# Two chained matmuls with a GELU: the opening's loads as eight of 512 KB, with a cast and turned by pairs of contraction slices

## The chip, the cores and the metric

The kernel runs on one core of one Trainium2 chip. The metric is the device time of one execution in microseconds (us); the kernel before is given by the median of 11 runs, 123.88 us (lowest 123.28, highest 124.94).

## The reference

a is 1024 x 1024, b is 1024 x 2048, c is 2048 x 1024, all float32.

```python
h = np.matmul(a, b)
h = 0.5 * h * (1 + np.tanh(np.sqrt(2 / np.pi) * (h + 0.044715 * h ** 3)))
return np.matmul(h, c).astype(np.float32)
```

## The kernel before, in words

TensorE contracts over the 128 partitions, so both operands need the contraction index there. b has it so as it lies in memory. a has its rows there, and must be turned: 128 x 128 blocks go through TensorE against an identity matrix into a PSUM bank, and VectorE copies them out to aT. The product is kept transposed: `hT[h][:, t]` is the GELU of 128 columns of b (tile t of 16) against 512 rows of a (half h of 2). The contraction has eight slices of 128 (k = 0 to 7).

The first product is computed in two parts. Its tiles t = 0 to 7 are plain bf16 matmuls (`mm1`, L109 to L112; each has 128 x 128 weights from b and 512 columns of aT). Its tiles 8 to 15, and the whole second product with c, go through `seven`, a seven-product scheme of sums and differences in float32r. Nothing of `seven` is changed here; it follows the part that is.

**The opening** is everything before the sixteen plain tiles can run freely. Slices k = 0 to 3 of a and of b's first 1024 columns are fetched in float32 by SyncE's queue into the staging buffers sta and stb, and cast to bf16 on the chip. All the rest (a's slices 4 to 7, called a2; b's slices 4 to 7; the second half of b; c) is fetched by GpSimd's queue, which casts to bf16 on the way. GpSimd's queue is held back by the gate (L81): a copy of one element of stb, which can only run when the load that brings this element has landed, and GpSimd takes its work in order.

The parts that matter here, in the order in which each engine gets them (the schedule is written out by hand, and every engine runs its own list in order):

- SyncE: sixteen loads of 256 KB with rows of 2 KB. Four of a (half 0, one block of 128 rows each, 512 columns), b's slices 0 and 1 (columns 0 to 511, called c = 0), four of a (half 1), b's slices 2 and 3, and then b's slices 0 to 3 for columns 512 to 1023 (c = 1). The gate reads slice 3, c = 0: the twelfth load.
- `turn1(h, fill)` (L125 to L137): for each block m of 128 rows, cast (VectorE for even m, ScalarE for odd), four transposes into bank 4 + m, a few small matmuls on zeros (`stir`, L119 to L123), and copies of 128 x 512 to aT. Only after all four blocks is aT for that half complete, for all four slices at once.
- `cast_b(k, c)` (L139 to L142): ScalarE casts one slice of b to b1.
- The plain matmuls of tiles 0 to 3: half 0 with slices 0 and 1 (8), `turn1(1)`, half 1 with slices 0 and 1 (8), and then both halves with slices 2 and 3 (16): 32 in all, in banks 0 to 7. Then `half` (L162 to L167): ScalarE and VectorE copy the eight partial sums to SBUF, in turn.
- T2 (L238 to L251): tiles 4 to 7 of both halves, in banks 0 to 6, first with slices 0 to 3, then tile by tile with slices 4 to 7 and the GELU. Between the first ones, four `turn` calls transpose a2 into bank 7 (L173), and VectorE copies it out (L174). A T2 tile can start when its bank has been copied to `half`, and needs the c = 1 columns of b1.

Behind that stand the second halves of tiles 0 to 3 (L254 to L259), and `seven` twice.

Of the kernel before, what the change touches and what calls it, by code (L numbers as in the profile page):

```python
# [9 lines left out]
F32 = mybir.dt.float32  # L10
F32R = mybir.dt.float32r
BF16 = mybir.dt.bfloat16
AF = mybir.ActivationFunctionType
# [6 lines left out]
def kernel(ctx, tc, a, b, c, out):  # L20
    nc = tc.nc
# [3 lines left out]
    H = 512  # L25
    KT = K // 128
    NT = N // 128

    av = a.rearrange("(mt p) k -> p mt k", p=128)
    bv = b.rearrange("(kt p) n -> p kt n", p=128)  # L30
# [9 lines left out]
    def slot(tag, shape, dt, name):  # L40
        return big.tile(shape, dt, name=name, tag=tag)

    def bank(i, shape=(128, H), dt=F32, name="ps"):
        return pp.tile(list(shape), dt, name=name, tag=f"bank{i}", padded_shape=None)

    def pieces(tag, bufs, shape, dt, name):
        return small.tile(shape, dt, name=name, tag=tag, bufs=bufs)
# [3 lines left out]
    ident = consts.tile([128, 128], BF16, name="ident")  # L51
    make_identity(nc, ident)
    gate = consts.tile([128, 1], F32, name="gate")
# [4 lines left out]
    aT = slot("a", [128, 2, KT, H], BF16, "aT")  # L58
    b1 = slot("b1", [128, KT, 1024], BF16, "b1")
# [1 line left out]


    KH = KT // 2
    stb = slot("x0", [128, 4, 1024], F32, "stb")
    sta = slot("x1", [128, 2, 4, H], F32, "sta")

    def load_a(h, m):
        nc.sync.dma_start(out=sta[:, h, m], in_=av[:, 4 * h + m, 0:H])  # L68

    def load_b(k, c):  # L70
        nc.sync.dma_start(out=stb[:, k, ts(c, H)], in_=bv[:, k, ts(c, H)])

    for h in range(2):
        for m in range(4):
            load_a(h, m)
        load_b(2 * h, 0)
        load_b(2 * h + 1, 0)
    for k in range(KH):
        load_b(k, 1)

    nc.gpsimd.tensor_copy(gate, stb[:, 3, 0:1])  # L81
    nc.scalar.activation(g, warm[:, 0:1], AF.Gelu_apprx_tanh)
    wps = bank(7, name="warmps")
    for _ in range(7):
# [11 lines left out]
    for n in range(2):  # L96
        for k in range(0, KT, 4):
            nc.gpsimd.dma_start(out=b2[:, k:k + 4, ts(n, H)],
                                in_=bv[:, k:k + 4, ds(1024 + n * H, H)])
# [3 lines left out]
    def copy(eng, dst, src):  # L103
        if eng is nc.scalar:
            nc.scalar.activation(dst, src, AF.Copy)
        else:
            nc.vector.tensor_copy(dst, src)  # L107

    def mm1(p, t, h, ks, k0=0, k1=KT):  # L109
        for k in ks:  # L110
            nc.tensor.matmul(p, b1[:, k, ts(t, 128)], aT[:, h, k],  # L111
                             start=(k == k0), stop=(k == k1 - 1))  # L112

    def gelu(t, h, p):
        nc.scalar.activation(hT[h][:, t], p, AF.Gelu_apprx_tanh)  # L115

    ps = {(0, t): bank(t) for t in range(4)}

    def stir(n):  # L119

        for _ in range(n):
            nc.tensor.matmul(ps[0, 3][:, 0:128], warm[:, 0:128], warm[:, 0:128],
                             start=True, stop=True, skip_group_check=True)  # L123

    def turn1(h, fill):  # L125
        pts = []
        for m in range(4):
            ab = pieces("ab", 4, [128, H], BF16, "ab")
            copy(nc.scalar if m % 2 else nc.vector, ab, sta[:, h, m])
            pt = bank(4 + m, (128, KH, 128), BF16, "pt")  # L130
            for k in range(KH):
                nc.tensor.transpose(pt[:, k], ab[:, ts(k, 128)], ident)  # L132
            stir(fill[m])
            pts.append(pt)
            if m in (0, 2, 3):
                for q in ((0,), (), (1, 2), (3,))[m]:
                    nc.vector.tensor_copy(aT[:, h, 0:KH, ts(q, 128)], pts[q])  # L137

    def cast_b(k, c, n=1):  # L139
        for i in range(n):  # L140
            r = ds(c * H + i * (H // n), H // n)
            nc.scalar.activation(b1[:, k, r], stb[:, k, r], AF.Copy)  # L142

    turn1(0, (2, 0, 4, 5))
    for k in range(2):
        cast_b(k, 0, 2 - k)
        for t in range(4):
            mm1(ps[0, t], t, 0, (k,), 0, KH)
    turn1(1, (0, 0, 0, 0))
    for t in range(4):  # L150
        ps[1, t] = bank(4 + t)
    for k in range(2):
        for t in range(4):
            mm1(ps[1, t], t, 1, (k,), 0, KH)
    for k in range(2, KH):
        cast_b(k, 0)
        for h in range(2):
            for t in range(4):
                mm1(ps[h, t], t, h, (k,), 0, KH)


    half = slot("x3", [128, 2, 4, H], F32, "half")  # L162
    for k in range(KH):
        cast_b(k, 1)
    for h in range(2):
        for t in range(4):
            copy(nc.vector if t % 2 else nc.scalar, half[:, h, t], ps[h, t])  # L167

    def turn(h, m, i):
        pt = bank(i, (128, KH, 256), BF16, "pt")  # L170
# [67 lines left out]
    T2 = [(h, t) for h in range(2) for t in range(4, 8)]  # L238
# [4 lines left out]
            turn(n // 4, 2 * (n % 2), 7)  # L243
    one.t3()
    one.t2()
    for h, t in T2[:7]:
        mm1(ps[h, t], t, h, range(KH, KT))
        gelu(t, h, ps[h, t])
    p = bank(7)
    mm1(p, 7, 1, range(KT))  # L250
# [3 lines left out]
    for n in range(8):  # L254
        h, t = divmod(n, 4)
# [156 lines left out]
```

## Time and profile before

| | |
|---|---|
| median of 11 runs | 123.88 us |
| profiled execution, whole time | 124.3 us |
| its span (first to last instruction) | 122.5 us |
| TensorE busy | 113.3 us, 92% |
| VectorE / ScalarE / GpSimd busy | 87.9 / 55.1 / 14.8 us |
| mean granted TensorE clock | 0.984 |
| read from HBM / written | 20.97 MB / 4.19 MB |

The profile counts from the span's start. Groups of instructions are named by line, engine and operation, with output and input by the program's names. PE is TensorE's matmul side, PEld its weight load, DVE VectorE, ACT ScalarE, POOL GpSimd, SPq SyncE's DMA queue. In a timeline a row is a run of like instructions: start, length, what it is, and in brackets how long the engine had been idle and what ended that. In a table by stages each row is a stretch of time with each engine's busy time in it, the granted clock (PEclk, 1.00 is full speed), the mean share of the DMA engines' time and the bytes moved. TensorE's matmuls are pipelined: a 512-column matmul is listed with 379 ns or more, but follows the one before it after 216 ns at full clock, and after 427 ns at half clock; a transpose after 56 or 107 ns.

### The profile page before, as it was taken

To read this page: it belongs to the slowest core of one execution; us is meant where nothing else is said; L and a number is where in the kernel's file an instruction comes from. 1 tells how busy PE (TensorE), PEld (TensorE's weight loads), DVE (VectorE), ACT (ScalarE), POOL (GpSimd) and SP (SyncE) were. 2 spreads that over 40 slices of the span, in tenths; PEclk is the share of its full clock that TensorE was granted. 3 is DMA by queue.
4 is the path that set the end of the run, shared out by engine and by line. 5 is a ranking of instruction groups with operands and counts; after the bars stand their busy time and mean duration, and the time that the engine had idled before them with its cause. 6 is when DMAs were issued, how large, how long until landed. Compare 5 with 4: busy or idle time off the path is not lost.

```text
span 122.5 us, 1463 instructions
## 1 busy us (share of the span) xinstructions
PE 113.3 (92%) x540; PEld 72.8 (59%) x546; DVE 87.9 (72%) x97; ACT 55.1 (45%) x89; POOL 14.8 (12%) x27
## 2 busy tenths in 40 slices
PE   6849599999999999999999999999999999999970
PEld 2333344455444444688888544458888888888850
DVE  0251606948805799979669999969999997792490
ACT  4225956001745688956579634920003596100000
POOL 2000597444223100000000000000000000000000
PEclk9995999999999999999999999999999999999999
DMA  3799999999999999998000000044000001004595
GB/s 118 243 265 400 340 136 198 166 196 205 207 206 213 211 209 212 212 211 166 8 3 0 5 0 0 0 172 171 0 0 0 0 5 76 10 0 171 215 354 201
DMA packets 10566, 16.86 MB, mean 138 GB/s; under 512 B 832, under 2 KB 3904, under 8 KB 10560
## 3 DMA queue, kind: packets, MB, share of 16 engines
q0 software_dynamic: 5952, 8.39, 39.6%
q1 hardware_dynamic: 4608, 8.39, 19.3%
q8 instruction: 4, 0.07, 0.2%
q14 instruction: 2, 0.02, 0.0%
HBM read 20.97 MB, written 4.19 MB: 205 GB/s over the span
## 4 chain that ended last, share of the span: by engine, by line
PE 71%; DVE 11%; DMA 10%; issue 2%; SPq 1%; ACT 1%; DVEq 0%; ACTq 0%
PE ps L227 49%; PE ps L111 20%; DVE x L185 6%; DMA stb<-in_b_dram 5%; DMA out_dram<-ot 5%; DVE ot L273 2%; DVE half L107 2%; SPq L68 1%; PE pt L173 1%; DVE aT L137 1%; DVE ot L358 1%; PE pt L132 1%; DVE aT L174 0%; ACT u L268 0%; DVE ab L107 0%
## 5 line engine op out<-in xcount | busy, mean ns | idle before, releaser
L111 PE MATMUL ps<-aT,b 128*128 128x512 bf16 x125 | 30.1, 394 | 1.6 <-ACT b L142 0.9
L227 PE MATMUL ps<-x,s 128*128 128x512 f32 x128 | 29.6, 391 | 0.0
L227 PEld LDWEIGHTS ps<-x,s 128*128 128x128 f32 x128 | 24.0, 188 | 5.1
L111 PEld LDWEIGHTS <-b 128*128 128x128 bf16 x128 | 12.6, 101 | 16.4 <-issue 2.1
L227 PE MATMUL ps<-x,x 128*128 128x512 f32 x64 | 14.8, 389 | 0.0
L227 PE MATMUL ps<-c_sb,hT 128*128 128x512 bf16 x62 | 13.9, 379 | 0.1
L227 PEld LDWEIGHTS ps<-x,x 128*128 128x128 f32 x64 | 12.0, 188 | 2.5
L268 ACT ACTIVATE v<-ps 128x512 f32<-128x512 f32 x8 | 4.8, 599 | 17.1 <-PE ps L227 17.1
L115 ACT ACTIVATE hT<-ps 128x512 bf16<-128x512 f32 x12 | 6.8, 594 | 11.4 <-PE ps L111 11.4
L227 PE MATMUL ps<-x 128*128 128x512 f32 x48 | 11.3, 394 | 0.0
L227 PEld LDWEIGHTS <-hT 128*128 128x128 bf16 x64 | 6.2, 98 | 7.6 <-issue 0.3
L227 PEld LDWEIGHTS ps<-x 128*128 128x128 f32 x48 | 9.0, 188 | 2.0
L258 DVE TENSOR_TENSOR half<-ps,half 128x512 f32<-128x512 f32 x8 | 5.5, 692 | 5.5 <-PE ps L111 5.1
L185 DVE TENSOR_TENSOR x<-c_sb 128x1024 fp32r<-128x1024 bf16 x8 | 9.2, 1216 | 0.0
L273 DVE TENSOR_TENSOR ot<-ps,v 128x512 f32<-128x512 f32 x8 | 5.3, 686 | 4.6 <-DMA out_dram<-ot 3.8
L273 DVE TENSOR_TENSOR ot<-ps,u 128x512 f32<-128x512 f32 x8 | 5.3, 690 | 3.1 <-ACT u L268 3.1
L115 ACT ACTIVATE hT<-ot 128x512 bf16<-128x512 f32 x12 | 6.9, 624 | 1.1 <-DVE ot L273 1.1
L227 PE MATMUL ps<-aT,b 128*128 128x512 bf16 x31 | 7.0, 379 | 0.1
L101 POOL DMA_DIRECT2D c_sb<-in_c_dram x8 | 5.7, 713 | 11.0 <-DMA b<-in_b_dram 11.0
L268 ACT ACTIVATE p<-ps 128x512 f32<-128x512 f32 x8 | 4.7, 594 | 4.9 <-PE ps L227 4.9
L137 DVE COPY aT<-pt 128x512 bf16<-128x512 bf16 x8 | 3.3, 421 | 4.5 <-PE pt L132 4.5
L115 ACT ACTIVATE hT<-half 128x512 bf16<-128x512 f32 x8 | 5.0, 631 | 2.6 <-DVE half L258 2.6
(47 smaller groups left out, 117.5 us busy)
## 6 DMA issues: line engine op xcount, KB each, us to landing
c_sb<-in_c_dram POOLq DMA_DIRECT2D x8, 512.0 KB, 19.9
out_dram<-ot SPq DMA_DIRECT2D x16, 256.0 KB, 2.1
sta<-in_a_dram SPq DMA_DIRECT2D x8, 256.0 KB, 5.9
stb<-in_b_dram SPq DMA_DIRECT2D x8, 256.0 KB, 5.9
b<-in_b_dram POOLq DMA_DIRECT2D x4, 512.0 KB, 14.6
a<-in_a_dram POOLq DMA_DIRECT2D x4, 256.0 KB, 5.3
b<-in_b_dram POOLq DMA_DIRECT2D x4, 256.0 KB, 9.5
```

The costliest lines, as they stand in the source:

```text
L68: nc.sync.dma_start(out=sta[:, h, m], in_=av[:, 4 * h + m, 0:H])
L101: nc.gpsimd.dma_start(out=c_sb[:, t:t + 2], in_=cv[:, t:t + 2])
L107: nc.vector.tensor_copy(dst, src)
L111: nc.tensor.matmul(p, b1[:, k, ts(t, 128)], aT[:, h, k], start=(k == k0), stop=(k == k1 - 1))
L115: nc.scalar.activation(hT[h][:, t], p, AF.Gelu_apprx_tanh)
L132: nc.tensor.transpose(pt[:, k], ab[:, ts(k, 128)], ident)
L137: nc.vector.tensor_copy(aT[:, h, 0:KH, ts(q, 128)], pts[q])
L185: nc.vector.tensor_tensor(out=dst[:, r], in0=x[:, r], in1=y[:, r], op=op)
L227: nc.tensor.matmul(p[:, ds(c0, w)], l[:, k, ts(j, 128)], r[:, k, ds(c0, w)], start=(start and k == 0), stop=(k == self.kt - 1), skip_group ...
L258: nc.vector.tensor_tensor(out=half[:, h, t], in0=p, in1=half[:, h, t], op=ADD)
L268: nc.scalar.activation(st, p, AF.Copy)
L273: nc.vector.tensor_tensor(out=ot, in0=p, in1=st, op=ADD)
```

## The change

SyncE makes eight loads of 512 KB in place of sixteen of 256 KB. A load of a brings all four row blocks of a half for two contraction slices (256 columns: rows of 1 KB); a load of b brings two slices (rows of 2 KB). Their order: a half 0 slices 0 and 1; b slices 0 and 1; a half 1 slices 0 and 1; a half 0 slices 2 and 3; b slices 2 and 3; a half 1 slices 2 and 3; then the two loads of b's c = 1. I number them 1 to 8. The gate reads b's slice 3, c = 0, as before: now load 5.

a is cast in one instruction of 128 x 1024 per load (three on VectorE, one on ScalarE), turned by eight transposes into one bank, and copied out in one instruction of 128 x 1024. aT is so ready by pairs of slices. The matmuls of tiles 0 to 3 follow in that order: half 0 with slices 0 and 1 (8), half 1 tiles 0 to 2 with slice 0 (3) and 1 (3), half 0 with slices 2 (4) and 3 (4), half 1 tiles 0 to 2 with slices 2 and 3 (6), and half 1's tile 3 with all four (4), since bank 7 serves the turns until then. Half 0's sums leave for `half` before the last ten matmuls, on ScalarE behind all four casts of c = 1. In T2, the second parts of the first four tiles run slice by slice over the four tiles, not tile by tile.

The loads, the gate and the opening (the diff's core; the functions `load_a`, `load_b`, `cast_a`, `turn1`, `block` and `leave` are new or rewritten):

```diff
-    stb = slot("x0", [128, 4, 1024], F32, "stb")
-    sta = slot("x1", [128, 2, 4, H], F32, "sta")
-    def load_a(h, m):
-        nc.sync.dma_start(out=sta[:, h, m], in_=av[:, 4 * h + m, 0:H])
-    def load_b(k, c):
-        nc.sync.dma_start(out=stb[:, k, ts(c, H)], in_=bv[:, k, ts(c, H)])
-    for h in range(2):
-        for m in range(4):
-            load_a(h, m)
-        load_b(2 * h, 0)
-        load_b(2 * h + 1, 0)
-    for k in range(KH):
-        load_b(k, 1)
-    nc.gpsimd.tensor_copy(gate, stb[:, 3, 0:1])
+    stb = slot("x0", [128, 2, KH, H], F32, "stb")
+    sta = slot("x1", [128, 2, 2, 4, 256], F32, "sta")
+    def load_a(h, q):
+        nc.sync.dma_start(out=sta[:, h, q], in_=av[:, 4 * h:4 * h + 4, ds(q * 256, 256)])
+    def load_b(q, c):
+        nc.sync.dma_start(out=stb[:, c, 2 * q:2 * q + 2], in_=bv[:, 2 * q:2 * q + 2, ts(c, H)])
+    load_a(0, 0)
+    load_b(0, 0)
+    load_a(1, 0)
+    load_a(0, 1)
+    load_b(1, 0)
+    load_a(1, 1)
+    load_b(0, 1)
+    load_b(1, 1)
+    nc.gpsimd.tensor_copy(gate, stb[:, 0, 3, 0:1])
...
-    def turn1(h, fill):
-        pts = []
-        for m in range(4):
-            ab = pieces("ab", 4, [128, H], BF16, "ab")
-            copy(nc.scalar if m % 2 else nc.vector, ab, sta[:, h, m])
-            pt = bank(4 + m, (128, KH, 128), BF16, "pt")
-            for k in range(KH):
-                nc.tensor.transpose(pt[:, k], ab[:, ts(k, 128)], ident)
-            stir(fill[m])
...
+    def cast_a(h, q, eng):
+        ab = pieces("ab", 2, [128, 4, 256], BF16, "ab")
+        copy(eng, ab, sta[:, h, q])
+        return ab
+    def turn1(h, q, i, ab):
+        pt = bank(i, (128, 2, H), BF16, "pt")
+        for n in range(2):
+            for m in range(4):
+                nc.tensor.transpose(pt[:, n, ts(m, 128)], ab[:, m, ts(n, 128)], ident)
+        nc.vector.tensor_copy(aT[:, h, 2 * q:2 * q + 2], pt)
...
-    turn1(0, (2, 0, 4, 5))
-    for k in range(2):
-        cast_b(k, 0, 2 - k)
-        for t in range(4):
-            mm1(ps[0, t], t, 0, (k,), 0, KH)
-    turn1(1, (0, 0, 0, 0))
-    for t in range(4):
...
-    for k in range(2, KH):
-        cast_b(k, 0)
-        for h in range(2):
-            for t in range(4):
-                mm1(ps[h, t], t, h, (k,), 0, KH)
+    def block(h, tiles, ks):
+        for k in ks:
+            for t in tiles:
+                mm1(ps[h, t], t, h, (k,), 0, KH)
+    stir(7)
+    turn1(0, 0, 4, cast_a(0, 0, nc.vector))
+    stir(8)
+    cast_b(0, 0, 2)
+    cast_b(1, 0)
+    block(0, range(4), (0, 1))
+    turn1(1, 0, 5, cast_a(1, 0, nc.vector))
+    for t in range(3):
         ps[1, t] = bank(4 + t)
+    ab = cast_a(0, 1, nc.scalar)
+    block(1, range(3), (0,))
+    turn1(0, 1, 7, ab)
+    block(1, range(3), (1,))
+    cast_b(2, 0)
+    cast_b(3, 0)
+    ab = cast_a(1, 1, nc.vector)
+    block(0, range(4), (2,))
+    turn1(1, 1, 7, ab)
+    block(0, range(4), (3,))
     for k in range(KH):
         cast_b(k, 1)
...
+    def leave(h, t):
+        copy(nc.vector if t % 2 else nc.scalar, half[:, h, t], ps[h, t])
+    for t in range(4):
+        leave(0, t)
+    block(1, range(3), (2, 3))
+    ps[1, 3] = bank(7)
+    mm1(ps[1, 3], 3, 1, range(KH), 0, KH)
+    for t in range(4):
+        leave(1, t)
...
-    for h, t in T2[:7]:
-        mm1(ps[h, t], t, h, range(KH, KT))
+    for k in range(KH, KT):
+        for h, t in T2[:4]:
+            mm1(ps[h, t], t, h, (k,))
+    for n, (h, t) in enumerate(T2[:7]):
+        if n >= 4:
+            mm1(ps[h, t], t, h, range(KH, KT))
         gelu(t, h, ps[h, t])
```

More of the change, by code (lines that the diff above doesn't have):

```diff
@@ L123, in stir @@
                              start=True, stop=True, skip_group_check=True)
-    def turn1(h, fill):
-        pts = []
-        for m in range(4):
-            ab = pieces("ab", 4, [128, H], BF16, "ab")
-            copy(nc.scalar if m % 2 else nc.vector, ab, sta[:, h, m])
-            pt = bank(4 + m, (128, KH, 128), BF16, "pt")
-            for k in range(KH):
-                nc.tensor.transpose(pt[:, k], ab[:, ts(k, 128)], ident)
-            stir(fill[m])
[L134 to L137, printed above, removed]
+    def cast_a(h, q, eng):
+        ab = pieces("ab", 2, [128, 4, 256], BF16, "ab")
+        copy(eng, ab, sta[:, h, q])
+        return ab
@@ L139, in cast_b @@
+    def turn1(h, q, i, ab):
[4 more added lines that the diff above has]
+        nc.vector.tensor_copy(aT[:, h, 2 * q:2 * q + 2], pt)
     def cast_b(k, c, n=1):
         for i in range(n):
-            r = ds(c * H + i * (H // n), H // n)
-            nc.scalar.activation(b1[:, k, r], stb[:, k, r], AF.Copy)
-    turn1(0, (2, 0, 4, 5))
-    for k in range(2):
-        cast_b(k, 0, 2 - k)
-        for t in range(4):
-            mm1(ps[0, t], t, 0, (k,), 0, KH)
@@ L149 @@
-    turn1(1, (0, 0, 0, 0))
-    for t in range(4):
-        ps[1, t] = bank(4 + t)
-    for k in range(2):
-        for t in range(4):
-            mm1(ps[1, t], t, 1, (k,), 0, KH)
-    for k in range(2, KH):
-        cast_b(k, 0)
-        for h in range(2):
-            for t in range(4):
-                mm1(ps[h, t], t, h, (k,), 0, KH)
-    half = slot("x3", [128, 2, 4, H], F32, "half")
+            r = ds(i * (H // n), H // n)
+            nc.scalar.activation(b1[:, k, ds(c * H + i * (H // n), H // n)], stb[:, c, k, r], AF.Copy)
@@ L163 @@
+    cast_b(3, 0)
[3 more added lines that the diff above has]
+    block(0, range(4), (3,))
     for k in range(KH):
         cast_b(k, 1)
-    for h in range(2):
-        for t in range(4):
-            copy(nc.vector if t % 2 else nc.scalar, half[:, h, t], ps[h, t])
+    half = slot("x3", [128, 2, 4, H], F32, "half")
+    def leave(h, t):
+        copy(nc.vector if t % 2 else nc.scalar, half[:, h, t], ps[h, t])
+    for t in range(4):
+        leave(0, t)
```

## The prediction

> **What bounds the kernel now.** I read first the table by stages, cut where TensorE changes its state.
>
> ```profile
> core 0: us, PE busy (x) PEld busy (x) DVE busy (x) ACT busy (x) POOL busy (x), PEclk, DMA share, GB/s
> 0.00:9.33 9.33, 5.71 (x34) 2.88 (x34) 2.73 (x7) 3.11 (x6) 0.69 (x6) 1.00 0.68 212
> 9.33:12.74 3.41, 3.31 (x8) 1.19 (x9) 0.43 (x1) 1.87 (x5) 0.00 (x0) 0.50 1.05 398
> 12.74:15.27 2.53, 1.28 (x18) 0.94 (x16) 1.85 (x5) 2.40 (x5) 1.58 (x3) 1.00 0.91 336
> 15.27:20.45 5.18, 5.13 (x24) 2.34 (x25) 1.10 (x2) 2.94 (x6) 4.89 (x9) 1.00 1.11 159
> 20.45:28.77 8.32, 8.09 (x60) 4.52 (x60) 6.23 (x8) 0.75 (x2) 4.02 (x6) 1.00 1.13 187
> 28.77:118.65 89.88, 89.67 (x401) 60.95 (x403) 74.81 (x75) 44.07 (x70) 3.60 (x6) 1.00 0.47 104
> ```
>
> From 28.77 to 118.65 us TensorE is busy 89.67 of 89.88 us at full clock, and what follows its last matmul is a fixed tail. So the end moves with the moment at which TensorE gets into that run, and only time lost before 28.77 can be won. It is lost before 15.27 (idle, and a stage at half clock), with a little in 20.45 to 28.77. Next, TensorE's timeline there:
>
> ```profile
> 9.44 3.52 PE L111 MATMUL ps<-aT,b 128*128 128x512 bf16 x8 [0.85 <-ACT b L142]
> 12.79 0.61 PE L132 MATMUL pt<-ident,ab 128*128 128x128 bf16 x8
> 14.03 0.62 PE L132 MATMUL pt<-ident,ab 128*128 128x128 bf16 x8 [0.63 <-DVE ab L107]
> 15.27 7.93 PE L111 MATMUL ps<-aT,b 128*128 128x512 bf16 x35 [0.62 <-DVE aT L137]
> 24.69 0.61 PE L173 MATMUL pt<-ident,a 128*128 128x128 bf16 x8 [0.18 <-DVE aT L174]
> ```
>
> Eight of the 32 opening matmuls run at half clock (9.44 to 12.79: 427 ns each, not 216); half 1 is turned, aT comes at 15.27, and the other 24 take 24 x 0.216 = 5.18 us, so T2 starts at 20.45. The last row is the small later loss: the matmul before ends at 24.35, and the transposes wait 0.34 us for bank 7, because VectorE was in the 2.28 us L185 sum. Last, what feeds this:
>
> ```profile
> 8.96 1.27 ACT L142 ACTIVATE b<-stb 128x256 bf16<-128x256 f32 x3 [1.11 <-DMA stb<-in_b_dram]
> 12.99 3.95 ACT L142 ACTIVATE b<-stb 128x512 bf16<-128x512 f32 x6
> 19.14 2.07 ACT L105 ACTIVATE half<-ps 128x512 f32<-128x512 f32 x4 [2.20 <-PE ps L111]
> 13.69 0.32 POOL L81 COPY gate<-stb 128x1 f32<-128x1 f32 x1 [12.38 <-DMA stb<-in_b_dram]
> 13.95 2.97 POOL L92 DMA_DIRECT2D a<-in_a_dram  x4
> ```
>
> The six casts of the second row follow the loads as they land. The trace holds the completions of SyncE's sixteen loads: 3.33, 4.74, 6.32, 7.20, 8.94, 9.58, 10.25, 10.94, 11.60, 12.29, 12.97, 13.63, 14.32, 14.99, 15.64, 16.29 us. From the fifth on it is one per 0.67 us (391 GB/s, one 2 KB row per 84 ns on each of 16 DMA engines); before that it is slower, with a stall about 6 to 7 us. Of each load the slowest DMA engine is some 1.4 us behind the fastest.
>
> **What the Trainium skill says.** "DMA: Bandwidth & Descriptors", section "Why small descriptors are slow (HBM only)": each packet costs some 3 bus cycles beside its bytes; so 1 KB would cost 35 cycles against 67 for 2 KB, an estimate of 44 ns from this trace's 84. No row here shows a 1 KB read. The same page, "Queues, rings and completion order": a DMA engine goes round the queues that have work, so GpSimd's loads, once begun, share with SyncE's. The trace before doesn't show them together: SyncE's data ends about when GpSimd's begins. "TensorE: Matmul & The Clock Gate", Part 1: the clock is set by how busy TensorE was in windows of about 3.4 us. The trace agrees: it changes at 5.91, 9.33 and 12.74, 3.41 apart. A window with 0.95 us of work (5.91 to 9.33) led to half clock; one with 1.77 us (12.74 to 16.15) kept it full.
>
> **The change, part by part.**
>
> *Loads.* The same 4 MB come in the same queue, so I take the old completions at equal bytes. A row of 1 KB: this trace's casting packets take 98 ns when they read 2 KB and 173 ns for 4 KB, so 37.5 ns per KB and 23 fixed; SyncE's 84 ns for 2 KB leaves 9 fixed, so 46.5 ns (42 if proportional, 60.5 with 23 fixed). A load of a has 32 such rows per engine: 32 x (46.5 - 42) = 0.14 us more. Load by load: 1 at 4.9; 2 at 7.3 to 8.4 by how the stall falls (I take 7.6); 3 at 9.87; 4 at 11.37; 5 at 12.72; 6 at 14.2; 7 at 15.57; 8 at 16.87. Eight issues instead of sixteen on SyncE (0.43 us each) win nothing, since landing, not issuing, is waited for.
>
> *The gate.* It opens at 12.75 in place of 13.69. Before, the first casting packet followed the gate's start by 2.2 us; now that is 15.0, with load 8 outstanding and its slowest engine having some 1.6 us of data left. Shared one to one from there, load 8 slips by up to 1.6 us; not at all if SyncE's packets go first. Nothing shows which; I take 0.6, so load 8 at 17.45. The casting loads gain some 0.5 us; the nearest need is b's slice 7 (landed 29.02, used 29.42), which now has the slice-by-slice order of T2 as well, 12 matmuls or 2.6 us later. No loss there. c's last load lands at 59.35, its first use is at 66.2: covered.
>
> *Casts, turns and copies.* A cast of 128 x 1024 isn't in the trace; VectorE's 128 x 512 takes 0.43 and a second half at most that: 0.67 to 0.86, I take 0.75. ScalarE: 0.41 for 256 and 0.63 for 512 columns give 1.07. The copy out of a bank, 0.68 (the L174 row's like). Turning stays at 32 transposes of 56 ns. All lies beside loads, except the chains below.
>
> *TensorE's path.* b's first casts end 0.44, 0.74 and 1.29 us after load 2, as now after the fifth load, so the first eight matmuls end at 9.8 at full clock. Load 3: cast to 10.65, turned at 11.15, copied at 12.1; three matmuls to 12.8. Load 4: ScalarE's cast to 12.45, turned 12.8 to 13.25, copied at 14.15; three matmuls of half 1 lie beside that. Slices 2 and 3 of b are cast at 14.03. Four matmuls 14.2 to 15.05; load 6 (cast to 14.97) is turned 15.05 to 15.5, copied at 16.4, beside four more matmuls. Then ten matmuls: 16.45 to 18.6. So TensorE is through at 18.6, not 20.45: only ten matmuls are left when the last of aT is there, not 24.
>
> *ScalarE's path.* T2's first tile takes bank 0, which `leave(0, 0)` empties on ScalarE, behind all casts of c = 1. Before, each of these landed by itself and one cast was left after the last; now load 8 brings two: 2 x 0.65, the copy 0.6, and some 0.15 of signalling: 2.05 us after load 8, so 17.45 + 2.05 = 19.5. This is later than TensorE's 18.6, and is the new bound: T2 starts at 19.5.
>
> *Sum.* 20.45 - 19.5 = 0.95 us. VectorE's L185 sum now begins at about 19.3 to 20.2 and ends before the first a2 copy is wanted (T2's start + 12 x 0.216 + 0.45 = 22.5), so the 0.34 us wait goes as well; the 0.08 us waits behind the next two turns stay (0.69 us copy against a 0.86 us gap). In all 1.3 us: 124.3 becomes 123.0 for the profiled execution, which lay 0.42 above the median; the median 123.88 becomes 122.6.
>
> **The rivals.**
>
> *Rows of 1 KB cost more (slower).* Every load from the first carries it: 4 x 32 rows x (d - 42) ns on load 8. Forecast with d = 46.5. The gain of 1.3 us is used up at 46.5 + 1300/128 = 56.7 ns; at 60.5 the time is 123.88 + 0.5 = 124.4; if a row costs 84 whatever its length, 3.5 us slower than before, 127.4. For it: 23 ns fixed on the casting queue. Against: SyncE's own 84 ns leaves room for 9 only, if bytes cost the same.
>
> *The queue share is full, or nearly.* Load 8 at 18.5, T2 at 20.5, only the 0.34 us won: 123.6, no change that can be told. For it: the gate falls 1.7 us of data before SyncE's end. Against: the fast DMA engines are done by then, and only the slow ones have both.
>
> *The clock.* Between 9.33 and 12.74 TensorE would work 1.1 to 1.5 us, between the 0.95 that lost the clock and the 1.77 that kept it. At half clock from 12.74 to 16.15, the path above ends at 19.9 instead of 18.6: 0.4 beyond ScalarE's, 123.0.
>
> *Better.* No sharing and proportional rows: load 8 at 16.3, T2 at 16.3 + 2.05 = 18.4, so 2.05 + 0.34 won: 121.5.
>
> **How the numbers follow.** What this kernel's measurement can tell from no change is about 0.5%, 0.62 us. The forecast (122 to 123.1, with the clock rival's small price in it) gets 0.55; better than that, 0.07; the full share, 0.25 (a third of it still under 123.26, since the slip has all values up to 1.6); rows slow enough to be slower than before, 0.13 (above 124.5, 0.10). Faster 0.64, within 0.5% 0.26, slower 0.10. The range 121.6 to 124.2 leaves out the extreme of the gain and most of the slow rows.
>
> **What would show it.** The stage before T2 shorter by about 1 us; ScalarE in one run of casts and copies just ahead of T2's first matmul, with TensorE idle before it by up to 1 us; the bank-7 wait gone; the packets of a near 46 ns. Wrong: TensorE busy right up to T2 (then its own path binds); load 5 later than 13.3 (rows dear); PEclk at 0.5 in 12.7 to 16.2.

## The result and the profile after

The changed kernel takes 120.69 us (median of 12 runs, 120.50 to 120.75) against 123.75 (median of 47, 122.61 to 125.01): ratio 0.9755, 95% interval 0.9734 to 0.9776. It is faster by 3.1 us, where 1.3 was forecast and the forecast's range reached down to 121.6. The spread shrank from 2.4 us to 0.25. The profiled execution took 120.69, its span 118.9 (before: 124.3 and 122.5). Where executions of one kernel lie more than 1.5% apart, which happens with several of the experiments, I give the median and the range of all of them, but every ratio is taken from the executions within 1.5% of the fastest of their kernel.

First the table by stages of the changed kernel, cut where TensorE's work changes as before.

```profile
core 0: us, PE busy (x) PEld busy (x) DVE busy (x) ACT busy (x) POOL busy (x), PEclk, DMA share, GB/s
0.00:9.33 9.33, 7.88 (x45) 4.41 (x46) 2.35 (x4) 2.73 (x5) 0.69 (x6) 1.00 0.81 254
9.33:12.74 3.41, 2.44 (x19) 1.29 (x18) 1.46 (x3) 2.21 (x3) 1.59 (x3) 1.00 1.07 369
12.74:14.82 2.08, 2.06 (x17) 0.96 (x15) 1.36 (x3) 0.88 (x2) 2.08 (x5) 1.00 1.10 333
14.82:16.97 2.15, 2.15 (x12) 0.97 (x10) 1.83 (x3) 1.97 (x5) 1.90 (x5) 1.00 1.24 204
16.97:25.04 8.07, 8.02 (x61) 4.52 (x61) 5.63 (x6) 1.39 (x3) 4.11 (x7) 1.00 1.15 196
25.04:114.91 89.87, 89.66 (x401) 60.90 (x403) 74.89 (x75) 43.54 (x70) 4.28 (x6) 1.00 0.49 107
```

The long run (25.04 to 114.91) is as long as before, 89.87 us, only 3.73 us earlier. T2 starts at 16.97 in place of 20.45: 3.48 us. T2's first part (16.97 to 25.04) is 0.25 us shorter than its 8.32 before: the 0.34 us wait for bank 7 is gone. No stage is at half clock from 6.69 us on, where the trace's record of the clock begins; before that the transposes still follow one another at 107 ns. The timeline of TensorE:

```profile
7.16 1.90 PE L112 MATMUL ps<-aT,b 128*128 128x512 bf16 x8 [0.26 <-ACT b L141]
8.93 0.62 PE L135 MATMUL pt<-ident,ab 128*128 128x128 bf16 x8
10.33 0.81 PE L112 MATMUL ps<-aT,b 128*128 128x512 bf16 x3 [0.78 <-DVE aT L136]
10.97 0.61 PE L135 MATMUL pt<-ident,ab 128*128 128x128 bf16 x8
11.64 1.75 PE L112 MATMUL ps<-aT,b 128*128 128x512 bf16 x6
13.41 0.62 PE L135 MATMUL pt<-ident,ab 128*128 128x128 bf16 x8
13.87 5.85 PE L112 MATMUL ps<-aT,b 128*128 128x512 bf16 x26
```

The first eight matmuls now take 1.90 us, not 3.52. The last turn ends at about 13.9, its copy at 14.77, and from 13.87 on the matmuls run on into T2 with no gap over 0.1 us. ScalarE, VectorE and GpSimd at the same place:

```profile
15.27 1.15 ACT L141 ACTIVATE b<-stb 128x512 bf16<-128x512 f32 x2 [0.18 <-DMA stb<-in_b_dram]
16.32 2.04 ACT L106 ACTIVATE half<-ps 128x512 f32<-128x512 f32 x4
14.07 0.69 DVE L136 COPY aT<-pt 128x1024 bf16<-128x1024 bf16 x1 [0.71 <-PE pt L135]
11.15 0.19 POOL L82 COPY gate<-stb 128x1 f32<-128x1 f32 x1 [9.85 <-DMA stb<-in_b_dram]
11.28 2.98 POOL L93 DMA_DIRECT2D a<-in_a_dram  x4
```

ScalarE's copy out of bank 0 ends at 16.91, 0.06 us before T2 starts: its path and TensorE's end together. The completions of SyncE's eight loads are 4.32, 6.67, 8.16, 9.70, 11.11, 12.57, 13.92 and 15.25 us. The forecast had 4.9, 7.6, 9.87, 11.37, 12.72, 14.2, 15.57 and 17.45. Here is the difference.

### The profile page after: what moved, and what is told of

The parts are those of the page before. It is cut to its first block, busy times and chain, and to the rows that moved or that the text cites. A ratio compares the mean times of both kernels' runs of the same rounds, so it can differ in the third digit from the quotient of the medians.

```text
span 118.9 us, 1452 instructions
## 1 busy us (share of the span) xinstructions
PE 112.4 (95%) x544; PEld 73.0 (61%) x550; DVE 88.3 (74%) x92; ACT 52.7 (44%) x86; POOL 14.6 (12%) x27
## 4 chain that ended last, share of the span: by engine, by line
PE 77%; DMA 10%; DVE 7%; issue 1%; ACT 1%; SPq 0%; DVEq 0%; ACTq 0%
PE ps L241 51%; PE ps L112 23%; DMA out_dram<-ot 5%; DMA stb<-in_b_dram 5%; DVE x L199 4%; DVE ot L291 2%; PE pt L187 2%; PE pt L135 1%; DVE aT L136 1%; DVE ot L376 1%; ACT u L286 1%; ACT b L141 0%; SPq L68 0%; DVEq L291 0%; DVEq L376 0%
## 5 line engine op out<-in xcount | busy, mean ns | idle before, releaser
L112 PE MATMUL ps<-aT,b 128*128 128x512 bf16 x124 | 28.8, 379 | 1.4 <-DVE aT L136 0.8
L112 PEld LDWEIGHTS <-b 128*128 128x128 bf16 x128 | 12.1, 98 | 15.0 <-issue 1.5
L241 PE MATMUL ps<-c_sb,hT 128*128 128x512 bf16 x62 | 13.9, 379 | 0.1
L116 ACT ACTIVATE hT<-ps 128x512 bf16<-128x512 f32 x12 | 6.3, 603 | 11.0 <-PE ps L112 11.0
L141 ACT ACTIVATE b<-stb 128x512 bf16<-128x512 f32 (+1 forms) x9 | 4.7, 573 | 6.6 <-DMA stb<-in_b_dram 6.6
L241 PE MATMUL ps<-aT,b 128*128 128x512 bf16 x32 | 7.1, 379 | 0.0
## 6 DMA issues: line engine op xcount, KB each, us to landing
c_sb<-in_c_dram POOLq DMA_DIRECT2D x8, 512.0 KB, 20.6
```

The source lines that it names most:

```text
L112: nc.tensor.matmul(p, b1[:, k, ts(t, 128)], aT[:, h, k], start=(k == k0), stop=(k == k1 - 1))
L141: nc.scalar.activation(b1[:, k, ds(c * H + i * (H // n), H // n)], stb[:, c, k, r], AF.Copy)
L241: nc.tensor.matmul(p[:, ds(c0, w)], l[:, k, ts(j, 128)], r[:, k, ds(c0, w)], start=(start and k == 0), stop=(k == self.kt - 1), skip_group ...
```

## The experiments

The theory behind the first ones: the changed kernel's loads run better because they are fewer and larger (A). Rivals: a's rows and order do it (B), or the execution that I had measured before was a chance (C).

**Large loads in the old kernel, small loads in the new one.** The first run joins the old loads by pairs, the second cuts the new ones in two.

```diff
-        nc.sync.dma_start(out=sta[:, h, m], in_=av[:, 4 * h + m, 0:H])
+        nc.sync.dma_start(out=sta[:, h, m:m + 2], in_=av[:, 4 * h + m:4 * h + m + 2, 0:H])
...
-        nc.sync.dma_start(out=stb[:, k, ts(c, H)], in_=bv[:, k, ts(c, H)])
+        nc.sync.dma_start(out=stb[:, k:k + 2, ts(c, H)], in_=bv[:, k:k + 2, ts(c, H)])
...
-        for m in range(4):
+        for m in (0, 2):
             load_a(h, m)
         load_b(2 * h, 0)
-        load_b(2 * h + 1, 0)
-    for k in range(KH):
+    for k in (0, 2):
         load_b(k, 1)
```

> The kernel before with its sixteen loads joined by pairs into eight of 512 KB (two row blocks of a, or two slices of b, rows of 2 KB as before); casts, turns, matmuls and the gate's element as before. Theory A, the number of loads sets the pace (sixteen loads through eight completions, SyncE's later issues waiting for earlier landings): the eight completions come near those of the changed kernel, the last at 15.2 to 15.5 us in place of 16.29, and the time falls by 0.7 to 1.3 us to 122.4 to 123.0. Theory B, the shape of a's loads (rows of 1 KB over four row blocks) or their order sets it: the last completion stays at 16.0 to 16.4, time 123.4 to 124.0. Theory C, the landing curve differs from execution to execution by chance: anything between, and not like the changed kernel's.

```diff
-        nc.sync.dma_start(out=sta[:, h, q], in_=av[:, 4 * h:4 * h + 4, ds(q * 256, 256)])
+        for m in (0, 2):
+            nc.sync.dma_start(out=sta[:, h, q, m:m + 2],
+                              in_=av[:, 4 * h + m:4 * h + m + 2, ds(q * 256, 256)])
...
-        nc.sync.dma_start(out=stb[:, c, 2 * q:2 * q + 2], in_=bv[:, 2 * q:2 * q + 2, ts(c, H)])
+        for k in (2 * q, 2 * q + 1):
+            nc.sync.dma_start(out=stb[:, c, k], in_=bv[:, k, ts(c, H)])
```

> The changed kernel with each of its eight loads cut in two of 256 KB in the same order (a: two row blocks each, rows of 1 KB; b: one slice each); all else as changed. Theory A: the last load completes about 16.3 us, as before the change, T2 starts about 18.0, time 121.5 to 122.0. Theory B: the last completes at 15.2 to 15.5 and the time is 120.6 to 120.9.

Measured, against 123.79 for the kernel before, run beside them: 122.52 (122.11 to 122.60) with large loads in the old order, ratio 0.9885 (0.9849 to 0.9922); its last load ended at 14.82 us. And 122.18 (121.78 to 123.11) with small loads in the new order, ratio 0.988 (0.983 to 0.993); its last load ended at 16.73. So for the landings A holds, and B falls: with small loads the new order's last load lands no sooner than the old one's (16.29). For the time, the size of the loads alone wins 1.3 us and the new order alone 1.6; the two add up to 2.9 of the 3.1.

**Which loads?** Two ideas within A: many small loads hurt in the start-up (A1), or SyncE has to wait for one of eight completions to come free (A2). The changed kernel with only its first two loads cut, and with all but these two cut:

```diff
+        w = 2 if (h, q) == (0, 0) else 4
+        for m in range(0, 4, w):
+            nc.sync.dma_start(out=sta[:, h, q, m:m + w],
+                              in_=av[:, 4 * h + m:4 * h + m + w, ds(q * 256, 256)])
...
+        w = 1 if (q, c) == (0, 0) else 2
+        for k in range(2 * q, 2 * q + 2, w):
+            nc.sync.dma_start(out=stb[:, c, k:k + w], in_=bv[:, k:k + w, ts(c, H)])
```

> The changed kernel with only its first load of a and its first load of b cut in two of 256 KB (ten loads; the last two find the completions of the first two long free); the other six stay 512 KB. Theory A1, many small loads hurt while the queue starts up (in the traces with small loads, one DMA engine falls 2 to 4 us behind the fastest by the third to fifth load, and the distance never closes; with 512 KB loads it stays under 1 us): one engine straggles, the last load completes at 15.8 to 16.7, time 121.3 to 122.2 with a wide spread. Theory A2, it is SyncE waiting for one of eight completions before it may issue: nothing waits here, the last load at 15.2 to 15.4, time 120.6 to 120.8.

The other has `!=` for each `==`.

> The other way round: the first load of a and of b stay 512 KB, the other six are cut in two (fourteen loads, six of which wait for a completion to come free). A1: the start is over, no engine straggles, the last load completes at 15.2 to 15.6, time 120.6 to 120.9. A2: SyncE's issues wait for landings as with sixteen loads, the last load at 16.0 to 16.7, time 121.4 to 122.2.

Measured: 123.12 (121.90 to 123.60, 20 runs) with the first two cut, and 120.83 (120.60 to 120.99) with the six others cut, both against 123.50. The ratios are 0.9958 (0.9932 to 0.9983) and 0.9751 (0.9704 to 0.9799). That is clear for A1: only the first two loads matter, and cutting them loses four fifths of the whole gain. Against A2, with the six others cut SyncE does wait for landings (its tenth load is issued at 6.46 us, just after the second landed at 6.44), and this costs nothing. The stages of the start-up show it; the two last columns are the DMA engines' busy share and GB/s. With the first two loads cut:

```profile
1.50:3.50 2.00, 2.00 (x6) 0.76 (x5) 0.00 (x0) 0.72 (x2) 0.00 (x0) 1.00 0.77 250
3.50:5.50 2.00, 1.99 (x14) 1.23 (x13) 0.69 (x1) 0.00 (x0) 0.00 (x0) 1.00 0.53 142
5.50:7.50 2.00, 0.83 (x15) 0.65 (x12) 0.69 (x1) 0.00 (x0) 0.00 (x0) 1.00 0.85 230
```

And the changed kernel:

```profile
1.50:3.50 2.00, 2.00 (x6) 0.76 (x5) 0.00 (x0) 0.72 (x2) 0.00 (x0) 1.00 0.78 228
3.50:5.50 2.00, 2.00 (x15) 1.25 (x13) 0.69 (x1) 0.00 (x0) 0.00 (x0) 1.00 0.99 253
5.50:7.50 2.00, 1.74 (x16) 1.36 (x15) 0.69 (x1) 0.81 (x3) 0.00 (x0) 1.00 1.04 361
```

With small first loads the DMA engines are idle nearly half of 3.5 to 5.5 us, although SyncE had issued six loads by 3.7 and a seventh by 4.3. Some fall behind: the fastest had its part of b's first load 3.19 us before the slowest (0.70 in the changed kernel). Most of the distance lasts to the end (2.23 us), and the last load ends at 17.30.

**A's first load or b's?** The same edit for one of the two alone: first for b's, `w = 4` for every load of a; then for a's, `w = 2` for every load of b.

```diff
-        w = 2 if (h, q) == (0, 0) else 4
+        w = 4
...
-        w = 1 if (q, c) == (0, 0) else 2
+        w = 2
```

> The changed kernel with only its first load of b cut in two of 256 KB (nine loads); a's first load stays 512 KB. In the run with both first loads cut, a's two halves landed at 3.6 and 4.3 us with a distance of 0.5 us between the DMA engines, and the first of b at 7.8 with 3.2. If it is the size of the first load of b that makes one engine fall behind: the same here, the first of b's loads at 7.5 to 8.5, time 122 to 123.3. If it is a's: as the changed kernel, 120.6 to 120.9.

> The changed kernel with only its first load of a cut in two of 256 KB (nine loads). If it is the size of b's first load: as the changed kernel, 120.6 to 120.9. If it is a's, or the number of loads queued ahead of b's first: 122 to 123.3.

Measured, against 123.26: b's first cut, 122.67 (121.47 to 123.11), ratio 0.9893 (0.9813 to 0.9974); a's first cut, 124.61 (121.44 to 127.07, 18 runs), ratio 0.9874 (0.9821 to 0.9928). Both lie clear of the changed kernel's 0.9755 (0.9734 to 0.9776). The last loads ended at 17.04 and 16.92. My either-or falls: each of the two does it alone, and by the ratios each loses about half of the gain. In the profile of a's, an execution of 126.21 us, the DMA engines were busy 0.43 of 3.5 to 5.5 us at 105 GB/s, and the clock was lost as well: it was at half from 7.64 to 17.88. What keeps the engines from the issued loads in the start-up stays open.

**Chance.** The kernel before, once more.

> The kernel before, once more, for a second profile of its loads. If the straggling engine belongs to its sixteen loads: again one engine 2 us or more behind by the fifth load, the last load at 15.8 to 17.3. If the first profile showed a chance stall: distances under 1 us and the last load near 15.

Measured: 122.87. The engines lay 2.04 us apart at b's first load, closed up later, and the last load ended at 15.45, not 16.29. So the lag comes again, and its size differs by execution: the one from which I took the landings was one of the late ones (124.3, 0.55 above the median). Over all the profiles, the largest distance between the engines in the loads up to b's slice 1 is 2.1 to 4.1 us in the seven where a first load of a or b is 256 KB. It is 0.4 to 1.2 in ten of the eleven where these are 512 KB or more. The eleventh, an execution of 122.57 us with all eight loads of the changed kernel (under "T2's order" below), has 1.80, and its last load ended at 15.95. So large first loads make a lag small as a rule; they don't rule it out.

**Still fewer loads.** Five, in the old kernel (a by halves of 1 MB, c = 1 in one):

```diff
-        for m in range(4):
-            load_a(h, m)
-        load_b(2 * h, 0)
-        load_b(2 * h + 1, 0)
-    for k in range(KH):
-        load_b(k, 1)
+        load_a(h)
+        load_b(2 * h, 2, 0)
+    load_b(0, 4, 1)
```

> The kernel before with five loads: each half of a in one of 1 MB (rows of 2 KB), b's c = 0 in two of 512 KB, c = 1 in one of 1 MB. Fewer than eight loads bring nothing more if the gain is that no engine straggles: the last load completes at 14.6 to 15.0 as with eight (14.82), but the first turn waits for 1 MB of a, so the time is 122.3 to 123.0. If each load costs by itself: the last at 14.0 to 14.4.

Measured: 123.73 (122.62 to 124.92), no different from before. The last load ended at 14.29, the earliest of all. But the first turn waited until 5.73 us for its whole megabyte, and in the profiled execution (124.51) the clock stayed at half until 12.42. The forecast of the time failed; what counts is not the last load alone.

**The gate.** On load 3, to see the sharing of the queues:

```diff
-    nc.gpsimd.tensor_copy(gate, stb[:, 0, 3, 0:1])
+    nc.gpsimd.tensor_copy(gate, sta[:, 1, 0, 3, 0:1])
```

> The changed kernel with the gate on load 3 (a, half 1, slices 0 and 1) in place of load 5, so that GpSimd's casting loads begin some 2.9 us sooner and run beside SyncE's last loads. If the two queues share a DMA engine one to one: loads 6 to 8 slip, the last by 1.5 to 3 us, T2 starts that much later and the time is 122 to 123.5. If SyncE's packets go first or there is room beside them: the last load within 0.3 us of 15.25, time 120.5 to 120.9.

Measured: 121.93 (121.79 to 122.02), ratio 0.9848 (0.9819 to 0.9876), 1.2 us over the changed kernel. From TensorE's and ScalarE's timelines of that run:

```profile
16.65 1.15 ACT L141 ACTIVATE b<-stb 128x512 bf16<-128x512 f32 x2 [1.41 <-DMA stb<-in_b_dram]
18.33 1.02 PE L112 MATMUL ps<-aT,b 128*128 128x512 bf16 x4 [0.95 <-ACT half L106]
```

Load 8 ended at 16.63 instead of 15.25, and T2 waited for ScalarE. From 14.0 to 14.5 us the trace has 48 packets of SyncE's queue and 48 of GpSimd's: one to one. With the gate on load 5 the first casting packet came at 13.99, when SyncE's queue had 40 of its 3072 data packets left to start, and hardly anything was shared.

**T2's order.** Tile by tile, as before:

```diff
-    for k in range(KH, KT):
-        for h, t in T2[:4]:
-            mm1(ps[h, t], t, h, (k,))
-    for n, (h, t) in enumerate(T2[:7]):
-        if n >= 4:
-            mm1(ps[h, t], t, h, range(KH, KT))
+    for h, t in T2[:7]:
+        mm1(ps[h, t], t, h, range(KH, KT))
         gelu(t, h, ps[h, t])
```

> The changed kernel with T2's second parts tile by tile, as before the change. As the forecast had it, this order only guards against a late slice 7 of b: in the changed kernel's trace that slice landed at 25.97 us, and tile by tile it would be wanted at about 25.7, so TensorE waits 0.3 us and the time is 120.9 to 121.1. If the order is worth nothing: 120.6 to 120.8. If it matters more (GELUs later, banks later): it can only be faster without it, 120.3.

Measured: 121.29 (120.97 to 122.57, 4 runs), 0.6 over the changed kernel; the ratio, 0.9817 (0.9756 to 0.9877), overlaps the changed kernel's. In the profiled execution (the slowest) slice 7 of b landed at 27.56:

```profile
27.61 2.76 PE L112 MATMUL ps<-aT,b 128*128 128x512 bf16 x11 [0.92 <-DMA b<-in_b_dram]
```

But in this execution SyncE's loads were late too (the last at 15.95, where the changed kernel's profile has 15.25), and with them the gate and b's slices. So the order is a guard that is worth something once TensorE arrives early, 0.3 us in the fastest execution and 0.6 in the median; how much of it is the order stays open.

**The clock.** The old kernel with more small matmuls on zeros, and the new one with none:

```diff
-    turn1(0, (2, 0, 4, 5))
+    turn1(0, (5, 10, 10, 14))
```

> The kernel before with more of the small matmuls on zeros in its opening (5, 10, 10 and 14 in place of 2, 0, 4 and 5), so that TensorE works some 2.4 us of each 3.4 us window and keeps the full clock; loads and order as before. If the stage at half clock was a real part of what the change won: eight matmuls take 1.73 us instead of 3.35, half 1 is turned some 1.2 us sooner in such an execution (limited by the loads of half 1, the last at 12.29 us), and the median falls by 0.5 to 1.2 us, 122.6 to 123.3, with a smaller spread. If the loads hide it: 123.6 to 124.0.

```diff
-    stir(7)
     turn1(0, 0, 4, cast_a(0, 0, nc.vector))
-    stir(8)
```

> The changed kernel without the fifteen small matmuls on zeros of its opening. If they keep the clock: the first eight matmuls run at 427 ns and end near 10.4 us instead of 8.9, and the path behind them ends up to 1.5 us later, 120.9 to 122.2 and with a spread from execution to execution. If the turns and matmuls alone are enough for the clock: 120.5 to 120.8.

Measured, against 123.50: the old kernel 123.45 (122.83 to 124.93, 20 runs), ratio 1.0008 (0.9982 to 1.0035). The full clock (in its profile from 6.95 us) wins it nothing that can be told; there its first matmul, at 10.46, waited for b, which landed at 9.97. The new kernel without them: 123.79 (121.85 to 124.31, 5 runs), ratio 0.9889 (0.9823 to 0.9955): by the median the whole gain is lost, by the ratio about half of it. TensorE's timeline in the slowest of the five:

```profile
7.27 3.57 PE L112 MATMUL ps<-aT,b 128*128 128x512 bf16 x8 [0.78 <-DVE aT L136]
10.64 1.06 PE L135 MATMUL pt<-ident,ab 128*128 128x128 bf16 x8
12.48 1.44 PE L112 MATMUL ps<-aT,b 128*128 128x512 bf16 x3 [0.78 <-DVE aT L136]
```

All at half clock, until 16.53; its loads ended as in the changed kernel (15.25), and yet T2 started at 20.6. So with loads in time the opening needs the clock.

**What binds T2's start now.** ScalarE's last cast of c = 1 on VectorE:

```diff
-    for k in range(KH):
+    for k in range(KH - 1):
         cast_b(k, 1)
...
         leave(0, t)
+    copy(nc.vector, b1[:, 3, ds(H, H)], stb[:, 1, 3])
```

> The changed kernel with the last cast of c = 1 (slice 3) on VectorE, which has room there, so that ScalarE empties bank 0 some 0.5 us sooner. As the forecast had it, ScalarE's path is the bound of T2's start: T2 then starts sooner by 0.1 to 0.5 us and the time is 120.2 to 120.6. If TensorE's own path binds (its last ten matmuls end as T2 starts in the changed kernel's trace): nothing, 120.6 to 120.8.

Measured: 120.55 (120.48 to 120.67), within the noise of 120.69. ScalarE's copies began at 15.75, 0.57 sooner, and T2 at 16.92, 0.05 sooner, which is what load 6 had landed sooner. So TensorE's own path binds. The same with load 6's cast shared by two engines, and with each copy into aT cut in two besides:

```diff
+    ab = pieces("ab", 2, [128, 4, 256], BF16, "ab")
+    copy(nc.vector, ab[:, 0:2], sta[:, 1, 1, 0:2])
+    copy(nc.scalar, ab[:, 2:4], sta[:, 1, 1, 2:4])
...
+        for n in range(2):
+            nc.vector.tensor_copy(aT[:, h, 2 * q + n], pt[:, n])
```

> The changed kernel with the last cast of c = 1 on VectorE (as tried by itself) and the cast of load 6 shared, two row blocks on VectorE and two on ScalarE. TensorE's path behind load 6 binds T2's start: the cast takes 0.43 to 0.63 in place of 0.69 us and the first four transposes need VectorE's half first, so T2 starts 0.1 to 0.3 us sooner and the time is 120.3 to 120.5. If something else binds: 120.5 to 120.7.

> The same with each copy of a turn into aT cut in two, one per slice, so that a slice's matmuls need not wait for the other's. The first is out 0.26 us sooner; behind load 6 the four matmuls of half 0 cover most of it: 0 to 0.15 us less than the run without it, 120.2 to 120.5.

Measured: 120.62 (120.57 to 120.97) and 120.42 (120.27 to 120.51), ratio 0.974 (0.9694 to 0.9786). The last is the fastest of all, with T2 at 16.79; from the changed kernel it isn't told apart by the intervals. The traces show the step, though: T2 starts 4.4 us after load 6 has landed in the changed kernel and with the cast of c = 1 moved, 4.24 with load 6's cast shared, 4.16 with the copies cut as well. In the last trace TensorE runs without a gap from 13.21 us, before load 6's last copy: what is left there is work, and before that it waits for loads and their casts.

**First touch.** One small load of b at the start:

```diff
+    first = consts.tile([16, 128], F32, name="first")
+    nc.gpsimd.dma_start(out=first, in_=b.rearrange("(g r) n -> g r n", r=64)[:, 0, 0:128])
     nc.gpsimd.tensor_copy(gate, stb[:, 0, 3, 0:1])
```

> The changed kernel with one small load on GpSimd's queue at the very start, 16 rows of 512 bytes of b at distances of 64 rows, used for nothing. In the traces the packets of SyncE's first load of b are slow wherever it stands (at 4.0 to 5.5 us in the changed kernel, 84 ns grown to 126 to 145; 6 to 7 us before). If that is the first touch of b's memory and one touch of each 512 KB warms it: the dip shrinks, the last load completes 0.5 to 1 us sooner, 119.9 to 120.4. If it comes from the load's own rows, or from the moment: the dip stays, 120.6 to 120.9.

Measured: 120.78 (120.53 to 121.36), inconclusive: the small load's packets came only at 5.37 us, after SyncE's first ones of b. The dip at 4 to 5 us stayed, so the first touch is neither shown nor ruled out.

## Why the prediction was wrong, point by point

- *The bound, right.* The end moved with TensorE's entry into its long run, and nothing later took anything back: 3.48 us at T2's start and 0.34 at bank 7, of which 3.73 arrived at its last matmul.
- *The step that failed: "I take the old completions at equal bytes".* Load 6, which TensorE's path hangs on, was put at 14.2 and came at 12.57; load 8, with the share, at 17.45 and came at 15.25. I took the slow start over unchanged, and it came with the old kernel's small first loads: larger ones leave the DMA engines less far behind. The profile showed it: the 1.4 us between engines was in my text, but it holds only from the seventh load on; before that it was 0.5 to 2.9, largest at the fifth, and I didn't ask why. I had also only one execution, a late one: with the landings of the second profile (the twelfth load at 12.78, not 13.63) the same step puts load 6 at 13.36, still 0.8 late. By these two profiles about half of this error was the execution that I read, and half the size of the loads. The term is 1.63 us on the path that binds; on the one that I took for the bound it is 1.6 of 2.2, and the share of the queues is the other 0.6.
- *The price of 1 KB rows, right.* Forecast 46.5 ns, measured 46 (median of 2048 packets), 84 to 88 for b's. The slower rival had no part.
- *The gate.* The share taken as 0.6 us was next to nothing. The 2.2 us from the gate to the first casting packet were misread: in the trace before that packet starts 1.8 us after the gate does (15.50 and 13.69) and ends at 15.90; in the changed kernel it took 2.8. The mechanism is there, one to one, when the casting loads begin early enough (gate on load 3), but at load 5 they don't meet.
- *The clock.* It was full from 6.69 us. How much hangs on it wasn't seen: without the small matmuls the kernel lost 3.1 us by the median and 1.2 in the fastest execution, not the rival's 0.4.
- *TensorE's path behind load 6, right.* 18.6 - 14.2 = 4.4 us forecast; 16.97 - 12.57 = 4.40 measured, and in parts: the copy out of the bank done 2.2 us behind load 6 in both, then ten matmuls.
- *ScalarE's path.* 2.05 us behind load 8 forecast, 1.72 to T2 measured: back to back its casts are 0.54 apart; the 0.65 of the old trace was the loads' own rhythm, which I read as the cast's. So it is level with TensorE's path and not the bound, and TensorE was busy right up to T2, which the forecast had named as a sign of being wrong.
- *T2's order, right in kind* (a guard), and worth 0.3 to 0.6 us, not named in numbers.

With the measured completions the forecast's own steps give 12.57 + 4.4 = 16.97 on TensorE's path and 15.25 + 2.05 = 17.3 on ScalarE's, so T2 at 17.3 and a gain of 3.15 + 0.34 = 3.5 us on the profiled execution, where the last matmul came 3.73 us sooner. Of the 2.53 us by which the forecast's T2 (19.5) came too late, the landings are 1.6, the share of the queues 0.6 and ScalarE's path, priced too long, 0.33.

## What to carry to other kernels

A new list of loads doesn't inherit the landing times of the old: ask for each load how far the slowest DMA engine is behind the fastest, where this began, and whether a second execution shows the same. In this kernel it paid to make the first two loads 512 KB each; the six others could be 256 KB at no cost (120.83), and a first load of 1 MB kept its consumer waiting (123.73). And the clock kept by filler work won nothing here while the loads were late (ratio 1.0008), and half of the gain or more once they were in time: after a change, measure again the edits that seemed idle before.

## What the hardware showed that I had not expected

- Two loads of 256 KB in place of one of 512 KB at the very start leave the DMA engines busy only 0.43 to 0.53 of 3.5 to 5.5 us when a's is cut (0.96 at 198 GB/s when b's alone is, 0.81 at 172 GB/s when all eight are), against 0.99 at 253 GB/s in the changed kernel. The last load ends 1.5 to 2.1 us later.
- The clock follows how long TensorE is listed as busy in windows of 3.41 us (a table by stages over such a window gives it). In the traces of all eighteen runs, every window at half clock with 2.63 us or less left it there (in the run without the small matmuls twice, 6.29 to 13.12), and every one with 2.79 or more raised it. At full clock, 1.46 us or less lost it and 1.66 or more kept it; between these lie one window with 1.53, which kept it, and one with 1.59, which lost it. So it takes more work to get the clock than to keep it.
- GpSimd's first casting packet came 1.6 us after its issue when SyncE's queue had 191 packets left to start (before), 2.7 when it had 580 (changed), and 4.4 when it had 1226 (gate on load 3).
